# A decoder block on one core: the rows that two gates take from the next tile, written by ScalarE and VectorE instead of copied by transfers

## The chip, the cores and the metric

The kernel runs on one core of one Trainium2 chip. The metric is the device time of one execution, in microseconds; the time of a kernel is the median over its runs. Engines are named as the profile names them: PE (TensorE matmul), PEld (its weight loads), DVE (VectorE), ACT (ScalarE), POOL (GpSimd), SP (SyncE, whose queue issues every transfer of this kernel; the profile writes SPq).

## The reference

The input is 512 positions of 1024 channels, in float32. What matters here is the recurrent mixer (RG-LRU) with its gates:

```python
h = rmsnorm(x, norm1_g[l])
z = h @ w_in[l] + b_in[l]
z_glu, z_rx, z_rg, z_ga, z_gb = jnp.split(z, split_idx, axis=-1)
...
xb = causal_depthwise_conv(z_rx, lru_conv_w[l], lru_conv_b[l])      # 1280 channels
...
xh = xf.reshape(bsz, s, LRU_HEADS, LRU_BLOCK)                       # 16 heads of 80
r = sigmoid(einsum('bshi,hij->bshj', xh, wa).reshape(bsz, s, d) + ba)
i = sigmoid(einsum('bshi,hij->bshj', xh, wx).reshape(bsz, s, d) + bx)
log_a = -LRU_C * r * softplus(-lam)
a = exp(log_a)
bterm = sqrt(-expm1(2.0 * log_a)) * (i * xf)
h = associative_scan(a, bterm)                                      # h_t = a_t h_{t-1} + bterm_t
...
y_b = (hb * gelu(z_rg)) @ lru_w_out[l]
m = sigmoid(z_ga) * y_a + sigmoid(z_gb) * y_b
x = x + m @ w_mix_out[l]
h = rmsnorm(x, norm2_g[l])
x = x + (silu(h @ ffn_w1[l]) * (h @ ffn_w3[l])) @ ffn_w2[l]
return rmsnorm(x, norm_f_g)
```

`y_a` is the other mixer: a gated linear unit, a depthwise convolution of 31 taps, a layer norm and a projection.

## The kernel before

Channels lie on the 128 partitions and the 512 positions along the row, so a tile holds 128 channels of all positions. Float32 accuracy is had from pairs: a value is cast to a rounded high part (`h`, type float32r) by ScalarE, and the rest is subtracted (`l`) by VectorE or, for weights of the first stage, by GpSimd (`split_to`, cast L118, subtraction L114). A product is three matmuls: high by high, high by low, low by high.

The first stage, up to about 330 us of the span, computes the input projection (`in_mm`, 24 matmuls of 128x512 for each tile of 128 outputs, L438) and beside it the mixers. Its order is written by hand in one list, of which this is the first half:

```python
ORDER = """u0 u1 rx0 rx1 gb0 rx2 u2 g0 rx3 gb1 g1 u3 rx4 g2 gb2 r0 r1 u4 g3 rx5 rg0 g4 rx6 rg1 u5 r2 r3 g5 rx7
    gb3 rg2 rx8 g6 rg3 u6 r4 r5 g7 ...
```

`u` is a gated linear unit's tile (two projections), `rx` a tile of the recurrent input with its convolution of 4 taps (`rx`, evictions L670 and L673, taps L675, result `xb`, pair `xbh`, `xbl`), `g` the two gates of one tile (`gates`, L718), `r` the recurrence (`recur`: `mu` in PSUM L740, L741, scan L742), `rg`, `gb`, `ga` the other projections with their gelu (L755, product L756) and sigmoids (L749). The 31 taps of the depthwise convolution run on VectorE in between, a step at a time (L597), two tiles at once; ScalarE starts them (L594) and copies the finished ones (L600). A framework orders the instructions of each engine from this list by estimated costs and sets the waits; each engine and each queue then works strictly in that order. Tiles in PSUM are taken in turn from six banks, so a projection waits for the last reader of the bank that it gets.

Weights come in chunks: a load to one of four raw buffers (L145, for gates many small loads into a cleared buffer, memset L184, loads L189), a cast, a subtraction, and four chunks are kept ahead of the one in use. SyncE's queue also carries the loads and stores of sums of feed-forward weights that GpSimd makes in passing (`fws` loads L333, sums, `ft` stores L346).

A head has 80 channels and a tile 128, so the gate of a tile also needs channels of a neighbouring tile: `gate_pieces` lists them. Tiles are treated in two groups of five. In the first of each group (tiles 0 and 5, so gates `g0` and `g5`, the first and the sixth) the head that crosses the border needs the first 32 channels (`FEW`) of the next tile (1 and 6). They lie in one tile `ext`: rows 0 to 31 the high part, 32 to 63 the low part, 64 to 95 the high part again, against the weights' high, high and low part, so that one matmul of 96 rows replaces three. `ext_in(i)`, called at the end of `rx(i)`, fills these rows with transfers from `xbh` and `xbl` (L698), as it does for all the other borders (`ext1` to `ext4`, `ext6` to `ext9`). Transfers are issued by SyncE.

Of the kernel before, what the change touches and what calls it, by code (L numbers as in the profile page):

```python
# [8 lines left out]
F32 = mybir.dt.float32  # L9
# [29 lines left out]
FEW, MANY = 32, 112  # L39
# [42 lines left out]
def tile_block(ctx, tc, a, out):  # L82
# [15 lines left out]
    def pairt(name, dtype=F32R):  # L98

        return longt(f"{name}h", dtype), longt(f"{name}l", dtype)  # L100
# [7 lines left out]
    vec, act, pe, pool_e = nc.vector, nc.scalar, nc.tensor, nc.gpsimd  # L108
# [4 lines left out]
    def sub(eng, o, x, y):  # L113
        return eng.tensor_tensor(out=o, in0=x, in1=y, op=ALU.subtract)  # L114
# [425 lines left out]
    ab, e, s, s2, po, c4 = (sm[:, i, :] for i in range(6))  # L540
# [125 lines left out]
    xb, xbp = [], []  # L666

    def rx(j):
        ps = in_mm(RX + j)
        act.activation(ps, ps, AF.Identity, bias=b_in(RX + j))  # L670
        o = longt(f"xb{j}")
        lw = lambda s: pc("lru_conv_w", (KL - 1 - s) * NR + j)
        act.activation(o, ps, AF.Identity, scale=lw(0), bias=pc("lru_conv_b", j))  # L673
        for s in range(1, KL):
            vec.scalar_tensor_tensor(out=o[:, s:], in0=ps[:, : T - s], scalar=lw(s), in1=o[:, s:], op0=ALU.mult, op1=ALU.add)  # L675
        xb.append(o)
        p_ = pairt(f"xb{j}")
        split(f"xb{j}", o, vec, p_)
        xbp.append(p_)
        ext_in(j)  # L680
# [3 lines left out]
    ext = {}  # L684

    def ext_in(i):
        g5, i5 = i - i % 5, i % 5
        for j5 in range(5):
            for at_, nr, tl, r0 in pieces[j5][1]:
                if tl != i5:  # L690
                    continue
                key = g5 + j5
                if key not in ext:
                    ext[key] = pairt(f"ext{key}") if j5 % 2 else (longt(f"ext{key}", F32R),)
                src = [v[r0 : r0 + nr, :].bitcast(F32) for v in xbp[i]]
                places = [(0, at_, 0), (1, at_, 1)] if j5 % 2 else [(0, at_ + FEW * k, k % 2) for k in range(3)]
                for d, at0, k in places:
                    nc.sync.dma_start(ext[key][d][at0 : at0 + nr, :].bitcast(F32), src[k])  # L698
# [461 lines left out]
```

## Time and profile before

| | |
|---|---|
| median of 3 runs | 818.55 us |
| all runs | 817.93, 818.55, 819.12 us |
| span of the profiled execution | 817.8 us (the page gives no other time of it) |
| TensorE's mean granted clock in it | 0.997 |
| busy: PE, DVE, ACT, POOL | 800.2, 654.9, 448.4, 225.3 us |
| moved by transfers | 159.25 MB |

In the rows below, a group's or instruction's row gives its start in us from the span's start, its duration, the engine (SPq is SyncE's queue), the source line, what is written from what, the shape, and in square brackets the idle time of the engine before it with what ended that. A wait's row gives who waited for whom, the total in us, the number of times, and the longest. A row of a stretch gives the busy time of each engine in it, then the granted clock as a share of full speed, the busy share of the transfer engines, and GB/s.

### The profile page before, as it was taken

Reading aid. Unit: us, or ns where it says so; the run is one execution under the profiler, and the core shown is the slowest. Engines: PE = TensorE matmul, PEld = TensorE weight load, DVE = VectorE, ACT = ScalarE, POOL = GpSimd, SP = SyncE. Lnnn points to the kernel's source line nnn. Section 1 sums busy time; section 2 is a strip of 40 time slices with the busy share of each in tenths; the row PEclk is TensorE's granted clock in tenths of the full one; section 3 lists DMA queues with packets and bytes.
Section 4 is the critical chain, followed back from the end, with each engine's and each line's share of the span. In section 5 each row is a group of like instructions: output and inputs, shape, how many; then the busy total and the mean of one; then the engine's idle time right before and its main releaser. Section 6 shows DMA issues by size and latency. Waiting matters only on the chain.

```text
span 817.8 us, 11826 instructions
## 1 busy us (share of the span) xinstructions
PE 800.2 (98%) x4110; PEld 685.3 (84%) x4110; DVE 654.9 (80%) x1018; ACT 448.4 (55%) x633; POOL 225.3 (28%) x172
## 2 busy tenths in 40 slices
PE   8999999899999999999999999999999999999996
PEld 7988888678888888888888898999998888788885
DVE  4699899989989988787878869787877565779556
ACT  7546585977668855553336455364644222466443
POOL 3575766866765854000000042000000000000000
PEclk9999999999999999999999999999999999999999
DMA  6746466477675753456838524788787887796552
GB/s 195 206 127 163 128 172 201 125 191 201 180 207 166 210 177 113 126 169 217 262 117 245 155 92 149 249 251 268 227 238 207 272 266 266 277 316 206 180 168 103
DMA packets 189551, 159.25 MB, mean 195 GB/s; under 512 B 14407, under 2 KB 157171, under 8 KB 189491
## 3 DMA queue, kind: packets, MB, share of 16 engines
q1 hardware_dynamic: 189491, 158.50, 63.5%
q8 instruction: 32, 0.52, 0.3%
q14 instruction: 28, 0.23, 0.1%
HBM read 127.13 MB, written 28.31 MB: 190 GB/s over the span
## 4 chain that ended last, share of the span: by engine, by line
PE 68%; DVE 12%; DMA 10%; SPq 3%; ACT 3%; issue 2%; POOL 2%; DVEq 0%; POOLq 0%; ACTq 0%
PE z L438 24%; PE or L841 12%; PE fr L1017 9%; PE yb L438 7%; PE ya L438 5%; PE mxr L841 5%; PE f L438 4%; DVE cv L597 3%; DMA ows<-in_ffn_w_dram 3%; DMA raw_in<-in_w_in_dram 2%; DMA ot<-ows 2%; PE g L718 1%; DVE hl_f L114 1%; POOL hl_in L114 1%; DVE ows L114 1%
## 5 line engine op out<-in xcount | busy, mean ns | idle before, releaser
L597 DVE SCALAR_TENSOR_TENSOR cv<-u,par,cv 128x511 f32<-128x511 f32 (+16 forms) x240 | 162.4, 730 | 2.4 <-ACT cv L594 2.2
L114 POOL TENSOR_TENSOR hl_in<-raw_in,hl_in 128x1024 fp32r<-128x1024 f32 x52 | 125.6, 2422 | 81.2 <-ACT hl_in L118 80.3
L118 ACT CAST hl_in<-raw_in 128x1024 fp32r<-128x1024 f32 x52 | 54.2, 1043 | 10.9 <-PE z L438 6.5
L114 POOL TENSOR_TENSOR fws<-fws 128x256 f32<-128x256 f32 x60 | 47.8, 799 | 5.0 <-DMA fws<-in_ffn_w_dram 2.3
L991 POOL TENSOR_TENSOR hf<-h20h,h20l 128x512 f32<-128x512 f32 x1 | 1.3, 1271 | 163.5 <-DVE h20l L482 163.5
L118 ACT CAST hl_f<-raw_f 128x1024 fp32r<-128x1024 f32 x24 | 25.1, 1051 | 36.3 <-DMA raw_f<-in_ffn_w_dram 14.9
L438 PE MATMUL z<-h10h,hl_in 128*128 128x512 f32 (+1 forms) x112 | 42.6, 382 | 1.1 <-DVE h10l L482 0.6
L438 PE MATMUL z<-h11h,hl_in 128*128 128x512 f32 (+1 forms) x112 | 41.7, 374 | 0.0
L438 PE MATMUL z<-h16h,hl_in 128*128 128x512 f32 (+1 forms) x112 | 41.7, 374 | 0.0
L438 PE MATMUL z<-h13h,hl_in 128*128 128x512 f32 (+1 forms) x112 | 41.7, 374 | 0.0
L438 PE MATMUL z<-h14h,hl_in 128*128 128x512 f32 (+1 forms) x112 | 41.7, 374 | 0.0
L438 PE MATMUL z<-h15h,hl_in 128*128 128x512 f32 (+1 forms) x112 | 41.7, 374 | 0.0
L438 PE MATMUL z<-h17h,hl_in 128*128 128x512 f32 (+1 forms) x112 | 41.7, 374 | 0.0
L438 PE MATMUL z<-h12h,hl_in 128*128 128x512 f32 (+1 forms) x112 | 41.7, 374 | 0.0
L114 DVE TENSOR_TENSOR hl_ob<-raw_ob,hl_ob 128x1024 fp32r<-128x1024 f32 (+1 forms) x23 | 26.9, 1176 | 17.8 <-ACT hl_ob L118 17.7
L118 ACT CAST hl_ob<-raw_ob 128x1024 fp32r<-128x1024 f32 (+1 forms) x23 | 23.3, 1015 | 31.7 <-PE or L841 12.0
L114 DVE TENSOR_TENSOR hl_f<-raw_f,hl_f 128x1024 fp32r<-128x1024 f32 x24 | 32.9, 1380 | 9.5 <-ACT hl_f L118 9.4
L114 DVE TENSOR_TENSOR ows<-ows,ows 128x512 f32<-128x512 f32 x22 | 15.2, 690 | 19.6 <-DMA ows<-in_ffn_w_dram 15.3
L1017 PE MATMUL fr<-hs_0h,hl_ft 128*128 128x256 f32 x160 | 29.7, 284 | 0.9 <-ACT c L1029 0.9
L114 DVE TENSOR_TENSOR hl_ft<-raw_ft,hl_ft 128x1024 fp32r<-128x1024 f32 x20 | 24.4, 1219 | 5.3 <-ACT hl_ft L118 5.3
L114 DVE TENSOR_TENSOR hl_ot<-raw_ot,hl_ot 128x1024 fp32r<-128x1024 f32 (+1 forms) x17 | 20.1, 1190 | 10.6 <-ACT hl_ot L118 10.2
L438 PEld LDWEIGHTS z<-h10h,hl_in 128*128 128x128 f32 x112 | 21.4, 191 | 5.8 <-DVE h10l L482 0.9
(903 smaller groups left out, 2602.5 us busy)
## 6 DMA issues: line engine op xcount, KB each, us to landing
raw_in<-in_w_in_dram SPq DMA_DIRECT2D x52, 512.0 KB
raw_f<-in_ffn_w_dram SPq DMA_DIRECT2D x24, 512.0 KB
ows<-in_ffn_w_dram SPq DMA_DIRECT2D x22, 512.0 KB
ot<-ows SPq DMA_DIRECT2D x44, 256.0 KB
fws<-in_ffn_w_dram SPq DMA_DIRECT2D x80, 128.0 KB
ft<-fws SPq DMA_DIRECT2D x80, 128.0 KB
raw_ft<-ft SPq DMA_DIRECT2D x20, 512.0 KB
raw_ob<-in_ffn_w_dram SPq DMA_DIRECT2D x33, 256.0 KB
```

Source lines behind the costliest of these rows:

```text
L114: return eng.tensor_tensor(out=o, in0=x, in1=y, op=ALU.subtract)
L118: copy(h, full)
L438: pe.matmul(ps, l, r, start=i == 0, stop=i == n - 1)
L597: vec.scalar_tensor_tensor(out=acc[c][:, s:], in0=u[c][:, : T - s], scalar=dw(c, s), in1=acc[c][:, s:], op0=ALU.mult, op1=ALU.add)
L718: pe.matmul(ps, l, r, start=k == 0, stop=k == len(mms) - 1)
L841: pe.matmul(banks[i], l_[:, ts], r_, start=start and n == 0, stop=stop and n == 2, skip_group_check=again)
L991: pool_e.tensor_tensor(out=v, in0=h2p[c][0].bitcast(F32), in1=h2p[c][1].bitcast(F32), op=ALU.add)
L1017: pe.matmul(ps[:, HALVES[i]], lw[:, 4 * i + c, :], rx_, start=not (again or i or c or m), stop=bool(i and c == 3 and m == 2), skip_group_c ...
```

## The change

In `ext_in`, for the first gate of each group of five, the three transfers are replaced: ScalarE casts the 32 rows of `xb` twice, to rows 0 to 31 and to rows 64 to 95 of `ext`, and VectorE subtracts the first copy from `xb` and writes rows 32 to 63. Both read the float32 tile `xb`, not the pair made of it. This happens twice in the kernel, after `rx1` and after `rx6`. The other borders are copied as before. The change adds six lines, so a line of the kernel before behind it has a number larger by six in the changed kernel.

```diff
@@ -692,6 +692,12 @@
                 key = g5 + j5
                 if key not in ext:
                     ext[key] = pairt(f"ext{key}") if j5 % 2 else (longt(f"ext{key}", F32R),)
+                if j5 == 0:
+                    full, e = xb[i][:FEW, :], ext[key][0]
+                    act.copy(e[:FEW, :], full)
+                    act.copy(e[2 * FEW : 3 * FEW, :], full)
+                    sub(vec, e[FEW : 2 * FEW, :], full, e[:FEW, :].bitcast(F32))
+                    continue
                 src = [v[r0 : r0 + nr, :].bitcast(F32) for v in xbp[i]]
                 places = [(0, at_, 0), (1, at_, 1)] if j5 % 2 else [(0, at_ + FEW * k, k % 2) for k in range(3)]
                 for d, at0, k in places:
                     nc.sync.dma_start(ext[key][d][at0 : at0 + nr, :].bitcast(F32), src[k])
```

## The prediction

> **What bounds the kernel now.** I read the page's busy shares first, then who TensorE waits for, then TensorE's timeline about the one long wait, then the granted clock there, and last what the queues did in the same microseconds.
>
> ```profile
> span 817.8 us, 11826 instructions
> PE 800.2 (98%) x4110; PEld 685.3 (84%) x4110; DVE 654.9 (80%) x1018; ACT 448.4 (55%) x633; POOL 225.3 (28%) x172
> PE g L718 <- DMA ext<-xb6h: 4.3, 1, 4.3
> PE or L841 <- DVE ov L967: 1.3, 1, 1.3
> ```
>
> TensorE (PE) is busy for 98% of the span, so the time moves only by what TensorE waits for or by its clock. The third and fourth lines are the two longest entries of its waits. The longest is one wait of 4.3 us, by a gate's product (L718) on the copy of rows of `xb6h` into `ext5`: one of the transfers that the change removes. The first gate's copies come from `xb1`, and no such wait stands in the list; that half of the change can gain nothing directly.
>
> ```profile
> 159.48 0.39 PE L718 MATMUL g<-xb5h,hl_gate 128*128 128x512 f32 x1
> 164.18 0.76 PE L718 MATMUL g<-ext,hl_gate 96*128 96x512 f32 x1 [4.31 <-DMA ext<-xb6h]
> 166.45 0.63 PE L438 MATMUL z<-h10h,hl_in 128*128 128x512 f32 x1
> 172.40 0.39 PE L438 MATMUL z<-h10h,hl_in 128*128 128x512 f32 x1
> 177.84 0.39 PE L438 MATMUL z<-h10h,hl_in 128*128 128x512 f32 x1
> 155.00:159.00 4.00, 4.00 (x19) 3.33 (x18) 4.00 (x7) 3.49 (x5) 3.84 (x5) 1.00 0.78 214
> 164.20:167.40 3.20, 3.20 (x8) 2.52 (x9) 3.20 (x5) 1.38 (x3) 3.12 (x3) 0.50 0.14 27
> 167.40:172.00 4.60, 4.60 (x22) 3.77 (x21) 3.77 (x7) 3.28 (x4) 1.69 (x2) 1.00 0.85 257
> ```
>
> These are TensorE's timeline (start, duration, what) and a table of stretches, whose third number from the right is the granted clock. From 172.40 to 177.84 run 24 products of one projection: 0.227 us each at full speed. From the third product of gate 5 (159.48) to 172.40 there are 30 steps (5 of the gate, 1 to the next projection, 24 of it), which at that pace take 6.80 us; they took 12.92. So the one wait costs **6.1 us**: 4.3 of standing still and, as the clock of 0.50 for some 3.4 us shows, 1.7 of half speed behind it. That is the most the change can give: 0.75% of the time.
>
> **Why the copy is late.** It is the queue, not the copy.
>
> ```profile
> 155.49 0.62 ACT L118 CAST xb6h<-xb 128x512 fp32r<-128x512 f32 x1 [1.27 <-DVE xb L675]
> 156.84 0.52 POOL L184 MEMSET raw_gate<- 128x512 f32 x1
> 157.39 2.31 SPq L189 DMA_DIRECT2D raw_gate<-in_lru_wa_dram  x5
> 160.89 0.54 SPq L698 DMA_DIRECT2D ext<-xb6h  x1
> 162.11 1.22 SPq L698 DMA_DIRECT2D ext<-xb6h  x2
> 162.11 1.97 DMA ext<-xb6h
> ```
>
> The rows exist at 156.11 (cast), but SyncE's queue first waits for GpSimd's memset and issues seven loads of gate 6's weights, so the three copies leave from 160.89 on and the last lands at 164.08 (last line, from the chain). Writing the rows by ScalarE and VectorE takes them out of that queue.
>
> **The change, part by part.** In the built order TensorE's and GpSimd's instructions stand exactly as before; ScalarE gains four, VectorE two, SyncE loses six.
>
> *Gate 5's rows.* TensorE wants them 0.227 us behind 159.48, at 159.71. ScalarE's order is now: cast of `xb6h`, cast of the fourth weight chunk ahead, two copies 32x512. No 32x512 copy is in the trace; between bounds
>
> ```profile
> 151.16 0.28 DVE L194 CAST hl_gate<-raw_gate 32x256 fp32r<-32x256 f32 x1
> 153.18 1.04 ACT L118 CAST hl_in<-raw_in 128x1024 fp32r<-128x1024 f32 x1
> 157.17 0.68 DVE L114 TENSOR_TENSOR xb6l<-xb,xb6h 128x512 fp32r<-128x512 f32 x1
> ```
>
> 0.28 (32 partitions, half as long, other engine) and 0.62 (the cast above, as long, four times the partitions) I take 0.6, since the 128x512 subtraction and cast agree and the column count is what stays. Then even without any earlier start the copies end by 156.11 + 1.04 + 1.2 = 158.4. VectorE's subtraction stands one convolution step behind `xb6l`: 157.17 + 0.6 + 0.65 + 0.6, near 159.0 at the latest. Both are ahead of 159.71. The 6.1 us go. The weight cast that slid behind `xb6h` ends near 157.1 instead of 154.2; its reader on GpSimd started only at 157.3 (memset, above, ends 157.36), so that costs nothing unless it slides further.
>
> *What is late next, first place.* The product after gate 5 (z of the eighth recurrent input, 166.45 above) now comes at 159.48 + 6 x 0.227 = 160.84. Its PSUM bank is the one of the third recurrence's `mu`, and the program makes it wait for the scan that reads that:
>
> ```profile
> 161.50 1.21 DVE L742 TENSOR_TENSOR_SCAN xb<-ea,mu 128x512 f32<-128x512 f32 x1
> 87.77 0.28 DVE L194 CAST hl_gate<-raw_gate 32x256 fp32r<-32x256 f32 x1 [2.08 <-POOL hl_gate L114]
> 99.19 0.59 ACT L600 COPY u<-cv 128x512 f32<-128x512 f32 x1 [5.19 <-DVE cv L597]
> 101.19 0.59 ACT L600 COPY u<-cv 128x512 f32<-128x512 f32 x1
> 102.50 4.73 DVE L597 SCALAR_TENSOR_TENSOR cv<-u,par,cv 128x511 f32<-128x511 f32 x7 [1.36 <-ACT cv L594]
> ```
>
> Before, the scan ended at 162.71 with TensorE arriving at 166.45: hidden. VectorE works without a gap from 102.5 to there; the new order has one convolution step (0.64) fewer ahead and the new subtraction (0.6) more, so the scan does not move by that. It moves a little by another reordering: at 99.19 ScalarE stood idle for 5.19 us before the copy of a finished convolution, with a sigmoid and a 1.04 us cast queued between the two copies; now both run in that idle time, the second copy ends near 101.2 instead of 101.78, and VectorE resumes some 0.5 us earlier. The first gate's own subtraction (0.6 at 62) is swallowed by a VectorE wait of 2.08 us at 87.8. Scan end: 162.2 (bounds 161.5 and 163.3). **New wait: 1.4 us** (0.7 to 2.5).
>
> *Its clock.*
>
> ```profile
> 708.99 0.93 PE L841 MATMUL or<-hl_ob,os1p 128*128 128x512 f32 x3 [1.26 <-DVE ov L967]
> 709.00:712.00 3.00, 3.00 (x13) 2.51 (x14) 2.97 (x6) 2.58 (x5) 0.00 (x0) 1.00 0.86 305
> ```
>
> A gap of 1.26 us leaves the clock at 1.00, one of 4.31 halves it. 1.4 is by far nearer to the first: no price taken; the other end is 3.4 us at half speed, 1.7. The Trainium skill, "TensorE: Matmul & The Clock Gate", in "A second HAM failure mode: psum-queue depth-cycling", speaks against the change here: short idling of TensorE between groups of products that cycle through PSUM banks, it says, made the clock swing between half and full. By that rule one such wait could cost the 1.7 and the sum below would be 2.4, not 4.1; the 1.26 row gives nothing, and I follow the row.
>
> *What is late next, second place: SyncE.* Gate 6 needs rows of `xb7`, still by transfers, and the new order has all four loads of w1 sums (`fws`) ahead of them where one stood.
>
> ```profile
> 173.04 1.91 SPq L333 DMA_DIRECT2D fws<-in_ffn_w_dram  x4
> 174.99 2.56 SPq L346 DMA_DIRECT2D ft<-fws  x4
> 177.65 2.23 SPq L189 DMA_DIRECT2D raw_gate<-in_lru_wa_dram  x4
> 180.28 0.39 SPq L333 DMA_DIRECT2D fws<-in_ffn_w_dram  x1
> 181.92 0.59 SPq L698 DMA_DIRECT2D ext6l<-xb7l  x1
> 189.63 0.40 PE L718 MATMUL g<-ext6l,hl_gate 112*128 112x512 f32 x1
> ```
>
> Three copies fewer put the queue 1.9 us ahead (0.61 each), so `fws` starts at 171.1; one weight load (0.6) has slid behind it, so the `ft` stores end at 177.55 - 1.9 + 0.6 = 176.2. The next `fws` waited for those stores to land, 180.28 - 177.55 = 2.73 behind their last issue: 178.95. Four loads (1.9) and two gate loads (1.1) later the copies start, near 182.0, the third (`ext6l`) at 183.2; with the 1.97 above it lands at 185.2. TensorE, 6.1 - 1.4 = 4.7 ahead, wants it at 184.9; the copy is twice as large as the one that took 1.97, and four loads run just before it, so I take 185.5: **0.6 us more** (0 to 2.5).
>
> *Behind that.* VectorE must keep up for the later banks, and it had waits to give back:
>
> ```profile
> DVE xb L675 <- ACT xb L673: 3.8, 2, 2.6
> DVE g L729 <- ACT g L728: 2.9, 2, 2.1
> 300.95 0.70 DVE L756 TENSOR_TENSOR z<-xb,z 128x512 f32<-128x512 f32 x1 [2.63 <-ACT z L755]
> ```
>
> 6.7 us of VectorE's idle time from 160 to 262, and 2.6 at 301, end with ScalarE's evictions of TensorE's own products, so they shrink as TensorE comes earlier; that covers 4.1. I take nothing off; what is left to the last stage follows TensorE, since no other wait of TensorE behind 260 is over 1.3 us.
>
> **Sum.** 6.1 - 1.4 - 0.6 = 4.1 us. Against the profiled span: 817.8 - 4.1 = 813.7; the page gives no time of its own beside the span, and the median of the runs (818.55) lies 0.75 above it. **814.4 us.** A measurement of this kernel can tell about 0.2% (1.6 us) from no change.
>
> **Rivals.**
>
> *Neither new wait comes* (VectorE or SyncE run further ahead): 818.55 - 6.1 = 812.4. For: the scan's 1.4 needs VectorE to stay where it was, and other reorderings also favour it. Against: it works without a gap there. Chance 0.14.
>
> *Only one comes:* between 818.55 - 5.5 and 818.55 - 4.7, near 813.5. The second wait is 0.6 of an estimate that can be 1 off. Chance 0.2.
>
> *The short waits drop the clock.* If the clock follows idle time added up over a few microseconds and not one gap alone, 1.4 us could be enough: 1.7 more, 816.1. It decides from a first wait somewhere between 1.26 and 4.31. Against: the 1.26 row, and the two waits are 24 us apart. This is where the rule of the Trainium skill's "TensorE: Matmul & The Clock Gate" named above would lead. Chance 0.06.
>
> *The gain is given back* further on, by VectorE at a bank or by a load that no longer arrives in time: within 1.6 us of 818.55. For: 80% VectorE. Against: TensorE waits nowhere else from 40 to 260 (its list of waits for that stretch holds the first line above alone). Chance 0.1.
>
> *Slower: the stall moves to gate 6.* If the four `fws` loads wait for the stores not 2.7 but 7 us, `ext6l` lands at 189.6: TensorE stands 4.7 us there, the clock halves again (1.7), and with 4.7 gained before the sum is +1.7: 820.3. It decides from a landing near 189.5. For: the queue is in order, with the copies behind. Against: that wait was 2.73. Chance 0.05.
>
> **How the numbers follow.** My forecast (both short waits, 814.4, itself 812.8 to 815.8) has 0.45. Faster by over 0.2%: 0.45 + 0.14 + 0.2 + 0.06 = 0.85; the same 0.1; slower 0.05. The range takes in the forecast's bounds and the first three rivals, 812.2 to 816.6, and leaves 0.15 out above.
>
> **What would show it.** Right: in the changed profile the 4.3 us wait on `ext<-xb6h` is gone; a wait of 0.7 to 2.5 us stands at the projection after gate 5 (L438), ended by VectorE's scan; one under 1 us at gate 6, ended by `ext6l`; the clock stays 1.00 from 155 to 200; copies of 32x512 take about 0.6. Wrong: a wait on VectorE's or ScalarE's new writes at gate 5, a clock of 0.50 behind a short wait, or TensorE's waits behind 200 us grown by over 2 us.

## The result, and the profile after

| | changed kernel | kernel before | ratio, 95% interval |
|---|---|---|---|
| first comparison (8 and 8 runs) | 816.62 us (814.59 to 817.52) | 818.42 us (817.68 to 819.94) | 0.9976 [0.9965, 0.9986] |
| second (12 and 35) | 817.04 us (815.78 to 822.70) | 819.14 us (816.58 to 822.51) | 0.9986 [0.9970, 1.0003] |
| third (12 and 29) | 817.82 us (816.23 to 821.90) | 819.15 us (817.11 to 820.99) | 0.9984 [0.9968, 0.9999] |

By the medians the change makes the kernel faster by 1.3 to 2.1 us; the interval of the second comparison just takes in no change at all. The forecast was 4.1 us, 814.4 with a range up to 816.6; the median of the first comparison lies 0.02 us above that range. The sign was right and the places of the new waits too; the size was a third to a half of what was forecast.

The profiled execution took 816.11 us with a span of 814.3. In every run listed with both, the time is 1.7 to 1.9 us above the span. So the profiled execution of the kernel before (span 817.8) was one of about 819.6 us, above its median, and the "0.75" of the prediction compared two executions. The sum of the prediction is 818.55 less 4.1 all the same, so this slip did not move it.

First the busy shares of the changed kernel and TensorE's waits in it from 40 to 300 us (who waited for whom, total, times, longest):

```profile
PE 798.0 (98%) x4110; PEld 684.5 (84%) x4110; DVE 657.1 (81%) x1020; ACT 450.4 (55%) x637; POOL 226.6 (28%) x172
PE z L438 <- DVE xb L748: 2.4, 1, 2.4
PE g L724 <- DMA ext6l<-xb7l: 0.7, 1, 0.7
```

The 4.3 us wait is gone, and the two waits that were forecast in its place are there: 2.4 us on the third recurrence's scan and 0.7 on `ext6l`. The timelines of the same execution about gate 5, of ScalarE, VectorE, TensorE and SyncE in turn:

```profile
156.78 0.61 ACT L697 CAST ext<-xb 32x512 fp32r<-32x512 f32 x1
157.42 0.62 ACT L698 CAST ext<-xb 32x512 fp32r<-32x512 f32 x1
157.90 0.68 DVE L114 TENSOR_TENSOR ext<-xb,ext 32x512 fp32r<-32x512 f32 x1
162.35 1.21 DVE L748 TENSOR_TENSOR_SCAN xb<-ea,mu 128x512 f32<-128x512 f32 x1
159.81 0.39 PE L724 MATMUL g<-ext,hl_gate 96*128 96x512 f32 x1
163.61 0.50 PE L438 MATMUL z<-h10h,hl_in 128*128 128x512 f32 x1 [2.42 <-DVE xb L748]
187.32 0.50 PE L724 MATMUL g<-ext6l,hl_gate 112*128 112x512 f32 x1 [0.71 <-DMA ext6l<-xb7l]
184.94 0.55 SPq L704 DMA_DIRECT2D ext6l<-xb7l  x1
```

The new writes are done at 158.04 and 158.58, and TensorE reads the rows at 159.81 without waiting. The scan ends at 163.56, and the projection that gets its bank starts right behind it.

How much that is worth varies from one execution to the next. One stretch measures it free of the start and the last stage: from one product of the projection ahead of gate 5 to the same product of one near 228 us. TensorE's timeline of before, then of the changed kernel:

```profile
154.49 0.39 PE L438 MATMUL z<-h11l,hl_in 128*128 128x512 f32 x1
228.71 0.39 PE L438 MATMUL z<-h14h,hl_in 128*128 128x512 f32 x1
```

```profile
154.59 0.39 PE L438 MATMUL z<-h11l,hl_in 128*128 128x512 f32 x1
226.50 0.39 PE L438 MATMUL z<-h14h,hl_in 128*128 128x512 f32 x1
```

That is 74.2 and 71.9 us. Over three profiles in which gate 5's rows are still transfers (before, before_again, only_g0) it is 74.2, 74.3 and 74.1; over four of the changed kernel (after, after_again, after_timed, after_third) 71.9, 73.8, 71.5 and 72.5, mean 72.4. The mean gain in this stretch is 1.8 us, the difference of the first pair of medians. Behind it, the next 940 products, up to about 440 us, take 213.21 us in all of these profiles: nothing is given back there. Behind 440 us executions of one kernel differ again, above all near 705 us, where the clock was halved in before_again and after_again and not in the other five.

### The profile page after: what moved, and what is told of

Read it like the earlier page. It is cut to its first block, busy times and chain, and to the rows that moved or that the text cites. A ratio compares the mean times of both kernels' runs of the same rounds, so it can differ in the third digit from the quotient of the medians.

```text
span 814.3 us, 11825 instructions
## 1 busy us (share of the span) xinstructions
PE 798.0 (98%) x4110; PEld 684.5 (84%) x4110; DVE 657.1 (81%) x1020; ACT 450.4 (55%) x637; POOL 226.6 (28%) x172
## 4 chain that ended last, share of the span: by engine, by line
PE 73%; DMA 9%; DVE 8%; SPq 3%; POOL 2%; issue 2%; ACT 2%; POOLq 0%; DVEq 0%; ACTq 0%
PE z L438 23%; PE fr L1023 12%; PE or L847 12%; PE f L438 7%; PE yb L438 7%; PE ya L438 5%; PE mxr L847 5%; DMA ows<-in_ffn_w_dram 2%; DVE cv L597 2%; DMA raw_in<-in_w_in_dram 2%; POOL hl_in L114 2%; DMA ot<-ows 1%; DMA raw_f<-in_ffn_w_dram 1%; PE g L724 1%; DVE hl_f L114 1%
```

## The experiments

**The same two kernels once more.** No edit. First before, then the changed kernel.

> The kernel before, profiled a second time, since the prediction rests on one profile of it. If the 6.1 us about gate 5 are in every execution, TensorE waits 4.0 to 4.6 us there again, the clock is 0.50 for 3.4 us behind it, and the span is near 817. If the half speed is only in some executions (rival), the wait is there but the clock stays at 1.00 and the span is 1.5 to 2 us shorter, near 816.

> The changed kernel, profiled a second time. If VectorE's backlog and the queue make the two new waits, they are there again: 2.0 to 2.8 us at the projection after gate 5, ended by the scan, and 0.4 to 1.0 us at gate 6, ended by ext6l. If they were chance, one of them is gone or twice as long.

Measured: 822.36 and 820.60 us, one execution each. The waits come back to a tenth (4.3 on `ext`; 2.4 on the scan), but behind the scan's wait the clock is now at half. Stretches of 3.41 us of the first profile of the changed kernel, then of `after_again` and of `after_third` (below), with the bounds put at the moments at which the granted clock changes (length, busy time of PE and of the others; third from the right the granted clock):

```profile
158.99:162.40 3.41, 2.20 (x10) 1.34 (x8) 3.38 (x7) 3.38 (x5) 2.66 (x2) 1.00 0.09 13
162.40:165.81 3.41, 2.20 (x10) 1.82 (x11) 3.41 (x5) 3.40 (x5) 3.25 (x4) 1.00 0.19 39
165.81:169.22 3.41, 3.41 (x17) 2.83 (x16) 3.41 (x7) 3.38 (x5) 3.33 (x3) 1.00 0.66 187
```

```profile
159.06:162.47 3.41, 1.65 (x7) 0.87 (x6) 3.41 (x6) 3.38 (x5) 2.64 (x2) 1.00 0.13 22
162.47:165.89 3.42, 2.77 (x7) 2.19 (x8) 3.42 (x5) 3.39 (x6) 3.19 (x5) 0.50 0.15 30
165.89:169.30 3.41, 3.41 (x10) 2.64 (x9) 3.41 (x7) 3.06 (x4) 3.30 (x3) 0.50 0.76 236
```

```profile
160.07:163.48 3.41, 0.98 (x5) 0.51 (x4) 3.41 (x6) 3.38 (x5) 2.64 (x2) 1.00 0.12 24
163.48:166.90 3.42, 3.42 (x9) 2.68 (x10) 3.42 (x6) 3.40 (x5) 3.19 (x6) 0.50 0.23 52
166.90:170.31 3.41, 3.41 (x17) 2.81 (x16) 3.41 (x6) 2.23 (x4) 3.32 (x2) 1.00 0.99 310
```

It is the same wait of 2.4 us three times. In the first it falls on the border of two such stretches of 3.41 us, called windows from here on; TensorE is idle for 1.21 us of each, 35%, and the clock stays. In the second it is idle for 52% of one, and the next two run at half. In the third the whole wait lies in one window (71% idle), and the next one runs at half. All changes of the clock in one execution lie on one grid of 3.413 us, and the grid stands differently against the program each time.

**Each half of the change alone.** First the first gate's rows only, then the sixth's only:

```diff
-                if j5 == 0:
+                if j5 == 0 and i == 1:     # only_g0;  only_g5: i == 6
```

> Only the first gate's rows are written by the engines; the sixth gate's come by transfers. Theory: the whole effect comes from the sixth gate, so the time is that of before within 0.15%, and TensorE's wait on ext<-xb6h is 4.0 to 4.6 us as before. Rival (the first gate's extra instructions or its other order cost or gain something of their own): over 1 us away from before.

> Only the sixth gate's rows are written by the engines. The scheduler gives VectorE another order: two convolution steps more and the second mu product stand ahead of the scan that frees the bank for the next projection. Theory (the scan's place on VectorE sets what is given back): the scan ends near 164.1, the new wait is 3.3 us instead of 2.4, the time 1.0 us above the changed kernel's and 0.5 to 2.5 us below before. Rival (the wait is set by ScalarE's two copies): 2.4 us as with both. Rival (the gain is the sixth gate's alone and the order does not matter): the time of the changed kernel.

Measured: only_g0 819.07 us, 0.9993 [0.9979, 1.0007] of before; only_g5 820.78 us, 1.0016 [0.9996, 1.0035]. TensorE's waits from 40 to 300 us, first of only_g0, then of only_g5:

```profile
PE g L724 <- DMA ext<-xb6h: 4.1, 1, 4.1
```

```profile
PE z L438 <- DVE xb L748: 3.0, 1, 3.0
PE g L724 <- ACT mu L746: 0.9, 1, 0.9
PE g L724 <- DVE y1l L114: 0.2, 1, 0.2
```

The first gate's half does nothing by itself, as forecast. The sixth gate's half alone removes the 4.3 us wait and still gains nothing. In its order one more tap and the fourth recurrence's product stand ahead of the scan, and the new subtraction of the 32 rows takes 2.13 us there (158.18 to 160.31) instead of 0.68. Gate 5 waits 0.9 us, until that subtraction is done (the list names ScalarE's `mu`, which this product does not read), the wait at the scan is 3.0, and 6.8 us at half clock follow. So which of the orders the change lands in matters as much as the copies.

**The scan moved ahead, and the second copies out of SyncE's queue.** In `after_r2` the third recurrence goes ahead of `u5`; in `after_r2_q6` ScalarE also issues the copies of `xb7`'s rows into `ext6`; `before_r2` is the first edit on the kernel before; `after_timed` is the changed kernel on the same chip.

```diff
-... rg1 u5 r2 r3 g5 rx7
+... rg1 r2 u5 r3 g5 rx7
-                    nc.sync.dma_start(ext[key][d][...
+                    (nc.scalar if (key, i) == (6, 7) else nc.sync).dma_start(ext[key][d][...   # after_r2_q6 only
```

> The changed kernel once more, on the chip of the three kernels below, so that they can be set against it. Theory A (the gain is cut by VectorE's backlog at the scan, by SyncE's order and by the half clock that the short waits call up in a share of the executions): 0.997 to 0.999 of the kernel before, some 2 us faster or less, and a spread of 3 us or more between executions; in the profile the waits of 2.4 us on the third recurrence's scan and of up to 0.7 on ext6l. Rival B (the first result stands and only the other chip was slow): 0.9976 as in the first comparison, within 0.0005, with executions within 1 us.

> One word moved in the order: the third recurrence (r2) stands ahead of the linear unit u5, so VectorE runs its scan some 7 us earlier and its bank no longer holds up the projection after gate 5. Theory A: the 2.4 us wait on the scan goes; TensorE then reaches gate 6 some 2.4 us earlier while SyncE issues the copies of xb7's rows as late as now, so the wait on ext6l grows from 0.7 to about 3; the time stays within 1 us of the changed kernel (0.999 to 1.001 of it), and the half clock shows up behind ext6l instead. Rival B (the scan's bank is all that was in the way): 2.4 us less than the changed kernel, 0.997 of it, and no wait on ext6l over 1 us. Rival C (VectorE is full; what is moved ahead comes back at another bank): a new wait on VectorE of about 2 us within the next 20 us.

> As the kernel with r2 moved, and besides the two copies of xb7's rows into ext6 are issued by ScalarE, behind its cast of xb7h, instead of by SyncE behind four weight loads. Theory A: both new waits go, and with them the half clock behind them: 3.1 us less than the changed kernel on average, 0.996 of it, and about 5 us less than the kernel before (0.993 to 0.995); TensorE waits for nothing over 0.5 us from 150 to 190. Rival C (VectorE or ScalarE is full): a wait on either of about 2 us within 20 us, and no more than 1 us less than the changed kernel.

> The kernel before with r2 moved ahead of u5 and nothing else: the copies for gate 5 are transfers in SyncE's queue as before. Theory A: the wait on ext5's rows stays at 4 us with the half clock behind it, and the time is that of the kernel before within 0.2%: the order by itself is worth nothing as long as the copies are late. Rival D (the order alone gives what the kernel with both moved gives): 2 us or more less than the kernel before.

Measured: after_timed 817.04 us, 0.9986 [0.9970, 1.0003]; after_r2 816.65, 0.9968 [0.9950, 0.9985]; after_r2_q6 818.42, 0.9996 [0.9981, 1.0011]; before_r2 818.70, 0.9996 [0.9983, 1.0008]. Seven of after_timed's twelve executions lie from 815.8 to 817.2 and the rest from 818.5 to 822.7: the spread that theory A expected. Waits from 40 to 300 us of after_r2, then of after_r2_q6:

```profile
PE g L724 <- DMA ext6h<-xb7h: 1.5, 1, 1.5
PE g L724 <- DVE ext L114: 1.0, 1, 1.0
PE g L724 <- DMA ext6l<-xb7l: 0.7, 1, 0.7
```

```profile
PE z L438 <- DVE xb L748: 2.0, 1, 2.0
PE g L724 <- DVE ext L114: 1.0, 1, 1.0
PE g L724 <- DMA ext6l<-xb7l: 0.7, 1, 0.7
```

The scan's wait goes, and 3.2 us of others come: VectorE now writes gate 5's rows 1.0 us late, which no theory had forecast, and gate 6 waits 2.2 for `xb7`'s rows, as theory A said. The late rows have a cause of their own. GpSimd and VectorE in after_r2:

```profile
156.94 2.40 POOL L114 TENSOR_TENSOR hl_in<-raw_in,hl_in 128x1024 fp32r<-128x1024 f32 x1
157.74 2.14 DVE L114 TENSOR_TENSOR ext<-xb,ext 32x512 fp32r<-32x512 f32 x1
```

In this order the new subtraction begins while GpSimd is in a subtraction of its own and takes 2.14 us instead of 0.68; in after_r2_q6 it is the same. More of this below, under the first new wait. The two edits together, which theory A had 5 us below before, fail: a later scan, which frees the bank of the projection that starts at 207.67, then takes 2.0 us. Rival C had such a wait on VectorE, though within 20 us and not some 45 us behind gate 5; after_r2_q6 does not show whether VectorE is full or held up by that subtraction. The order alone (before_r2) is worth nothing while the transfers are late: its wait is 4.3 us. after_r2 has the best ratio of all, but it is not told apart from the changed kernel by these runs.

**The size of the wait and the clock.** `after_5taps` leaves out the last five taps of two tiles of the depthwise convolution; `after_more` puts one more product ahead of the scan.

```diff
-            for s in range(1, KC):
+            for s in range(1, KC - (5 if c0 == 2 else 0)):                  # after_5taps
         vec.tensor_tensor(out=mu, in0=xb[j], in1=mu, op=ALU.mult)
+        for _ in range(1 if j == 2 else 0):                                 # after_more
+            vec.tensor_tensor(out=shortt("spare"), in0=xb[j], in1=mu, op=ALU.mult)
```

> The changed kernel with the last five taps of the depthwise convolution left out for channel tiles 2 and 3 (ten VectorE steps), so that two steps fewer, 1.3 us, stand ahead of the third recurrence's scan. Theory W (the granted clock is set in windows of 3.41 us and halves for the next window when TensorE was idle for about 0.45 of one, 1.5 us): the wait on the scan shrinks from 2.4 to 1.1 us, too short to halve the clock in any phase, so no half clock behind gate 5; what TensorE gains there it may lose on ext6l, whose landing does not move (wait up to 2.0), and there the half clock may appear. Rival G (any gap over about 1 us can halve the clock by chance): half clock behind the 1.1 us wait in some executions. Time: 0.998 to 1.0 of the changed kernel on either.

> The changed kernel with one more 128x512 VectorE product (its result not used) in the third recurrence; the fourth recurrence's scan then goes first and holds the bank that the projection behind gate 5 gets, some 1.3 us later than now. Theory W: a wait of 3.7 us is over half of some window in every phase, so the clock halves behind it in every execution for 3.4 or 6.8 us: 1.3 + 1.7 to 3.4 us more than the changed kernel's undisturbed executions, less the 0.7 of ext6l that it hides; the fastest of the executions above 817.5 and the median 819 to 820.5, where the changed kernel on an equal chip has 815.8 and 817.0. Rival G (clock drops are chance, whatever the wait): 1.0 us more than the changed kernel, 818, with half clock behind that wait in some profiles only.

Measured: after_5taps 833.19 us, 1.0157 [1.0135, 1.0179]; after_more 819.29, 1.0001 [0.9983, 1.0018], its fastest execution 817.12. after_5taps is a miss as an experiment. With other taps the planner orders much else anew: gate 6 waits 4.3 us, the layer norm 4.0, and the scan's wait is 3.3 instead of 1.1. It tells nothing of a shorter wait, but that longer one is a case of its own: it fell on a border, 45% and 52% of two windows, and the clock stayed at 1.00. after_more does nearly what theory W says: a wait of 3.6 us, half clock for 3.4 us behind it, the median in the forecast range and the fastest execution 0.4 below its bound. One profile alone does not rule out rival G; the count over all profiles, below, speaks against it.

**Other work for TensorE in the meantime.** `gb3` ahead of gate 5 and `rg3` ahead of gate 6, with the change (`after_gb3`) and without it (`before_gb3`):

```diff
-... u5 r2 r3 g5 rx7 gb3 rg2 rx8 g6 rg3 u6 ...
+... u5 r2 gb3 r3 g5 rx7 rg2 rx8 rg3 g6 u6 ...
```

> The changed kernel in another order: the projection gb3 stands ahead of gate 5 and rg3 ahead of gate 6, so TensorE has 5.4 us of other work while VectorE reaches the scan and the copies land. Theory A (the remaining loss is the waits on VectorE's backlog and SyncE's queue, and the clock behind them): TensorE reaches gate 5 near 165, the scan (163.5) is done: no wait over 0.5 us from 155 to 175 and no half clock; the time 1.5 to 4 us less than the changed kernel, 0.992 to 0.996 of the kernel before. Rival C (VectorE is full, the gain is given back at the next bank): a wait of 2 us or more between 175 and 215 and no gain on the changed kernel.

> The kernel before, with transfers for all the borders, in the same other order as the last one. Theory A: its copies for gate 5 land at 164.1 in SyncE's old place, TensorE wants them near 165.2: the 4.3 us wait goes without any engine writes, and the time is within 1 us of the changed kernel in that order (0.992 to 0.997 of the kernel before). Rival Q (SyncE's queue issues them later in this order too): the wait on ext5's rows stays over 2 us and the time within 0.2% of the kernel before.

Measured: after_gb3 820.86 us, 1.0010 [0.9991, 1.0028]; before_gb3 820.84, 1.0015 [0.9998, 1.0032]. Waits from 40 to 300 us, first with the change, then without:

```profile
PE g L724 <- DMA ext6h<-xb7h: 3.3, 1, 3.3
PE g L724 <- DVE xb L748: 0.7, 1, 0.7
PE g L724 <- DMA ext6l<-xb7l: 0.2, 1, 0.2
```

```profile
PE g L718 <- DMA ext6h<-xb7h: 3.8, 1, 3.8
PE g L718 <- DMA ext6l<-xb7l: 0.8, 1, 0.8
```

Without any engine writes the wait on gate 5's rows is gone when TensorE comes 5.4 us later; the first copy is issued at 159.73 in this order, 1.2 us earlier than in before. But the whole stall moves to gate 6, with half clock behind it (6.8 and 3.4 us), and theory A's gain fails.

**The scan's bank taken away, TensorE's order kept.** `mu` of the third and fourth recurrence in SBUF, where the other tiles lie, instead of PSUM, whose banks TensorE writes (`after_mu`), with the copies for `ext6` on ScalarE's queue besides (`after_mu_q6`), on the kernel before (`before_mu`), and the changed kernel on the same chip (`after_third`).

```diff
-        mu = bank(f"mu{j}")
+        mu = (shortt if j in (2, 3) else bank)(f"mu{j}")
```

> The changed kernel with mu of the third and fourth recurrence in SBUF instead of PSUM, so that the projection behind gate 5 gets a bank that no scan holds; TensorE's order is unchanged. Theory A: the 2.4 us wait is gone; TensorE reaches gate 6 some 2.4 us earlier and waits there for xb7's rows, whose copies follow VectorE and SyncE: 0.7 + 0.5 to 2.4 us. Window rule: no half clock at gate 5; behind gate 6 in every phase from a wait of 3 us on, in none below 1.4. Time 0.5 to 2.5 us below the changed kernel on the same chip, 0.995 to 0.998 of the kernel before. Rival S (SyncE's queue alone sets gate 6): the wait at ext6h is 3 us with half clock behind it and the time is no better than the changed kernel's.

> As the last, and the two copies of xb7's rows into ext6 are issued by ScalarE. Theory A: neither new wait over 1 us from 155 to 190 us, and none behind them until 210, where VectorE is next (2.0 us were seen there with both taken away): 1 to 3 us below the changed kernel, 0.993 to 0.997 of the kernel before. Rival C (VectorE's backlog takes all back at the next bank): a wait of 2 to 4 us between 195 and 215, and the changed kernel's time.

> The kernel before, transfers as they were, with mu of the same two recurrences in SBUF. Theory A: the 4.3 us wait for ext5's rows stays, with half clock behind it in every execution (1.00 of some window or two parts over 0.5): the kernel before within 0.2%. Rival M (the two tiles in SBUF are a gain by themselves): 1 us or more below the kernel before.

> The changed kernel on the chip of the last three. Wait on the scan 2.4 us and ext6l 0.3 to 0.7 as in its three profiles so far; half clock behind the scan exactly if one window of 3.41 us holds over about 1.7 us of the wait. Time 0.997 to 0.9985 of the kernel before.

Measured: after_mu 818.90 us, 1.0000 [0.9987, 1.0013]; after_mu_q6 822.96, 1.0048 [1.0030, 1.0066]; before_mu 820.10, 1.0012 [1.0001, 1.0023], its wait at gate 5 4.4 us; after_third 817.82, 0.9984 [0.9968, 0.9999]. Waits from 40 to 300 us of after_mu, then of after_mu_q6:

```profile
PE g L724 <- DMA ext6h<-xb7h: 2.0, 1, 2.0
PE z L438 <- ACT g L730: 1.1, 1, 1.1
```

```profile
PE z L438 <- DVE xb L748: 3.5, 1, 3.5
PE g L724 <- DMA ext6h<-xb7h: 2.5, 1, 2.5
PE g L724 <- DMA ext6l<-xb7l: 0.7, 1, 0.7
```

The wait on the scan is gone in both and nothing is gained: 2.0 us come back at gate 6 and 1.1 at 210 us; with ScalarE issuing the copies it is 3.2 and 3.5. Theory A's gain on the changed kernel fails again, but these two kernels are no test of the bank alone, for the edit has a price on VectorE. Its rows in after_mu:

```profile
167.97 3.06 DVE L747 TENSOR_TENSOR mu<-xb,mu 128x512 f32<-128x512 f32 x2
170.96 5.58 DVE L748 TENSOR_TENSOR_SCAN xb<-ea,mu 128x512 f32<-128x512 f32 x2
```

The two products and two scans, all of whose inputs now lie in SBUF, take 8.6 us; with `mu` in PSUM the same four take 3.6 (only_g5). So the edit itself gives VectorE some 5 us more to do ahead of `xb7`'s rows. after_third does what the window rule said of it. No version tried beats the changed kernel beyond doubt.

## Why the prediction was right or wrong

**The old wait, 6.1 us: right.** In the five profiles of kernels that copy gate 5's rows by transfers ahead of `gb3`, TensorE waits 4.1 to 4.4 us there, with half clock behind it each time, for 3.4 us or (before_r2, before_mu) 6.8. Counted from start to start of TensorE's products it cost 6.1 to 6.3 us in the three of them with half clock for 3.4 us. That it was mostly the queue is in the prediction's rows: 4.8 us from the rows' being there (156.11) to the first issue (160.89), 1.97 for the last copy. before_gb3 does not tell the two apart.

**The new writes: right.** 0.61, 0.62 and 0.68 us against 0.6, done at 158.04 and 158.58 against 158.4 and 159.0, and no wait on them. That the subtraction took no longer was luck: the prediction did not ask what GpSimd does beside it. In four of the twelve profiles in which the engines write gate 5's rows (only_g5, after_r2, after_r2_q6, after_gb3) it took 2.13 to 2.19 us, and in the first three gate 5 waited 0.9 to 1.0 us. The first gate's half gains nothing by itself: only_g0.

**The first new wait: the place right, the size wrong.** This is the step that failed. TensorE is idle for 2.4 us. The forecast of 1.4 (0.7 to 2.5) was counted from start to start, and so counted the wait is 2.7: from the product at 159.81 to the one at 163.61 are five steps, 1.13 us at full pace, and they took 3.80. VectorE was to keep to the end a lead of 0.5 us won near 100 us, to have one tap fewer ahead, and to pay 0.6 for the new subtraction. Its timeline, with a row of GpSimd's, in before, then after:

```profile
110.63 2.40 POOL L114 TENSOR_TENSOR hl_in<-raw_in,hl_in 128x1024 fp32r<-128x1024 f32 x1 [4.29 <-ACT hl_in L118]
111.62 1.96 DVE L114 TENSOR_TENSOR xb4l<-xb,xb4h 128x512 fp32r<-128x512 f32 x1
149.21 0.69 DVE L729 SCALAR_TENSOR_TENSOR g<-ea,g 128x512 f32<-128x512 f32 x1
156.54 0.72 DVE L597 SCALAR_TENSOR_TENSOR cv<-u,par,cv 128x487 f32<-128x487 f32 x1
```

```profile
110.73 2.40 POOL L114 TENSOR_TENSOR hl_in<-raw_in,hl_in 128x1024 fp32r<-128x1024 f32 x1 [4.29 <-ACT hl_in L118]
111.20 2.47 DVE L114 TENSOR_TENSOR xb4l<-xb,xb4h 128x512 fp32r<-128x512 f32 x1
149.02 0.70 DVE L735 SCALAR_TENSOR_TENSOR g<-ea,g 128x512 f32<-128x512 f32 x1 [0.28 <-ACT g L734]
156.36 0.87 DVE L114 TENSOR_TENSOR xb6l<-xb,xb6h 128x512 fp32r<-128x512 f32 x1
157.15 0.72 DVE L597 SCALAR_TENSOR_TENSOR cv<-u,par,cv 128x487 f32<-128x487 f32 x1
158.51 0.71 DVE L597 SCALAR_TENSOR_TENSOR cv<-u,par,cv 128x487 f32<-128x487 f32 x1
159.25 0.69 DVE L114 TENSOR_TENSOR y1l<-z,y1h 128x512 fp32r<-128x512 f32 x1
```

The lead was won: VectorE resumes at 101.75 instead of 102.50. Most of it is lost at `xb4l`, which begins 0.42 us earlier than in before and ends 0.09 later, both times about 0.55 us behind the end of a subtraction of GpSimd's that was running when it began (113.03 in before, 113.13 in after). The same holds throughout: in the 18 profiles, from 20 to 330 us, a subtraction of VectorE's with both inputs in SBUF, of the `xb` pairs or the new rows, ended 0.54 to 0.56 us behind such a subtraction or sum of GpSimd's in 84 of the 84 cases in which it began in the middle of one (0.1 us or more from both its ends). Where GpSimd ran nothing beside it, it took 0.68 or 0.69 us (50 of 50). No edit tested it. So being earlier gained VectorE nothing at `xb4l`. At 149 us a wait of 0.28 on ScalarE takes more of the lead, and with the saved tap already behind it, it is 0.19 us (149.21 - 149.02) instead of 1.1 (0.5 and a tap of 0.64). "VectorE works without a gap" was read from before, where `xb4l`'s 1.96 us counted as work, and did not hold in the new order.

Then the subtraction costs more than its own 0.6. `xb6l`, now earlier, ends 0.55 us behind a sum of GpSimd's and holds VectorE 0.79 us (156.36 to 157.15) instead of 0.60, and both the subtraction (157.90) and `y1l` (159.25) start 0.03 us behind the end of the tap before them, where in before `xb6l` (157.17) starts 0.09 ahead of that end. The Trainium skill, "VectorE: DVE Perf Modes", section "Two Vector instructions with no wait between them", has a rule of this kind: some pairs start only when the earlier one is finished. These rows agree with such a hold; which pair is held was not tried. Lead and subtraction together make 1.4 us: the scan ends at 163.56, where 162.2 was forecast.

**Its clock, no price: wrong, through the size of the wait.** The rival named the mechanism (idle time added up over a few microseconds) with 0.06. Over the 18 profiles of this case, from 20 to 800 us and in windows of 3.41 us on the grid at full clock, TensorE idle for more than 53% of one is followed by half clock in 18 of 18; between 44 and 53% in 3 of 12; from 20 to 44% in 1 of 28, that one at 44%. So the point lies between 1.5 and 1.8 us within one window. A wait of 1.4 us could not have reached it: no price was right for the forecast wait. At 2.4 the phase decides, and it was paid in two of four profiles of the changed kernel: 0, 3.0, 0 and 1.7 us (after, after_again, after_timed, after_third), 1.2 on average. The two waits 24 us apart do not add up, as said. The row of 1.26 us on which the prediction leaned was a matter of phase as well: in after_again the same wait at 708 us stood in one window with another of 0.95 us, 65% idle together, and half clock followed.

**The second new wait: right in size, 0.7, 0, 0.3 and 0 us of idle time against 0.6 (0 to 2.5)**, or 1.0, 0, 0.6 and 0 from start to start, though both sides of it came 1.7 to 1.8 us later than forecast: TensorE at 186.6 and the copy's issue at 184.94.

**Nothing lost behind that: right**, by the equal 213.21 us.

Put together, from start to start and on average over the profiles: 6.2 for the old wait, less 2.8 for the scan's wait (2.7 and 0.1 for the first product behind it), less 1.2 for the clock, less 0.4 for the second wait, is 1.8, what the stretch gives; the medians give 1.3 to 2.1. Against the forecast the scan's wait costs 1.4 more and the clock 1.2. Of the rivals, the one that comes nearest in time is the one on the clock (816.1), which had 0.06; its mechanism was there in two of the four profiles. Only one wait came in the same two, but with the half clock behind it, and neither never; these two rivals, 0.34 together, left out that price.

What stands behind this wait is not shown. The four edits that took the scan's wait away found 3.1 to 6.7 us of others before 215 us (after_r2, after_r2_q6, after_mu, after_mu_q6; 3.2, 3.7, 3.1 and 6.7), so the next limit is near. But all four made VectorE slower as well: the new subtraction takes 2.14 us in the first two, and the products and scans of the moved tiles take 5 us more in the other two. Whether VectorE's work, SyncE's queue or VectorE's meetings with GpSimd bind there stays open. Less VectorE work with all else unchanged was not achieved (after_5taps), and no edit moved GpSimd's instructions out of the way.

## What to carry to other kernels

Before a wait is counted as gained, work out when the next thing in the same place is ready, and put its upper bound into the sum if its engine has no slack there; a lead seen 60 us earlier is no slack. When an edit moves an instruction, look at what another engine runs beside its new place: here a subtraction of 0.68 us took 2.14 beside one of GpSimd's. A wait has a second price in the clock, and it is a step and not a slope: compare each remaining wait with half of a clock window, and count the price by phase when it is longer. A program's short list of waits does not say how far behind the next engine stands: take one wait away and read the list again before planning the next edit.

## What the runs showed of the hardware

The granted clock changes only on a grid of 3.413 us that stands anywhere against the program. Full clock is lost when a window is idle for about half, and half clock lasts on when the half-speed window itself has idle time: with 19% or more in nine of nine cases, with 10% or less in none of 22 (from 20 to 800 us, as above). So one and the same 2.4 us wait cost 0, 1.7 or 3.0 us more, and a 3.3 us wait in after_5taps cost nothing more. The Trainium skill, "TensorE: Matmul & The Clock Gate", "Part 1: The HAM clock gate", states a free-running window of 3413 ns, which the traces show. Its advice, under "Why this matters for your kernels", is to avoid gaps of more than about 3 us; here 1.8 us within one window were enough each time, and the measurement decides.

A subtraction of VectorE's that reads two tiles in SBUF and begins in the middle of a subtraction or sum of GpSimd's ends 0.54 to 0.56 us behind it, 84 times of 84 here, whatever its own 0.68 us. Products and scans that were given a second input in SBUF (after_mu) became longer too, 8.6 us instead of 3.6.
